# One step of a hybrid diffusion backbone: the stages of the mixer in another order

## The chip, the cores and the metric

The kernel runs on one core of a Trainium2 chip. The metric is the device time of one execution in microseconds (us). The kernel before takes 1578.61 us, the median of three runs from 1577.85 to 1579.18.

A core has engines that work side by side, each through its own instructions in order: TensorE (PE) multiplies matrices into PSUM banks, VectorE (DVE) and ScalarE (ACT) work element by element, GpSimd (POOL) and the queue engine SP here mostly issue DMAs. An instruction waits until what it reads has been written and what it overwrites has been read. ScalarE computes its functions (exponential, sigmoid, square root, gelu) from tables, and changes the table by an instruction of its own.

## The reference

Two layers of one network are applied to 128 context tokens and 256 latent tokens, 384 rows of 1024 numbers. Each layer is a feed-forward half step, a mixer and a second half step, each behind a norm that is scaled and shifted by numbers from a conditioning vector (the modulation):

```
mod = silu(cond) @ w_ada + b_ada
h = rmsnorm(x, g[0]) * (1 + mod[:, 1]) + mod[:, 0]
x = x + 0.5 * mod[:, 2] * swiglu(h, w_ffn_in[0], w_ffn_out[0])
h = rmsnorm(x, g[1]) * (1 + mod[:, 4]) + mod[:, 3]
x = x + mod[:, 5] * mixer(h)
h = rmsnorm(x, g[2]) * (1 + mod[:, 7]) + mod[:, 6]
x = x + 0.5 * mod[:, 8] * swiglu(h, w_ffn_in[1], w_ffn_out[1])
```

The mixer projects h (1024 columns) to 2144 columns, which three groups of heads share:

```
qa, ka, va, xb, gb, cq, ckv, kr = split(h @ w_in)        # 256 256 256 512 512 192 128 32
A: q, k = rope(headnorm(qa)), rope(headnorm(ka));  o_a = subln(softmax1 - lam * softmax2) @ va
B: xc = dwconv(xb); r, i = sigmoid(gates(xc)); a = exp(-8 r softplus(-lam))
   h_t = a_t h_(t-1) + sqrt(1 - a_t^2) i_t xc_t, forward and backward;  o_b = (hf + hb) * gelu(gb)
C: q = rope(headnorm(rmsnorm(cq) @ w_uq)); k, v from rmsnorm(ckv) @ w_ukv and kr;  o_c = softmax(q k) @ v
out = concat(o_a, o_b, o_c) @ w_out
```

Context tokens attend to context alone, latent ones to 128 cached context keys and the 256 latent keys. Normed keys, values, latents and the last scan states of the context are outputs too.

## The kernel before

The tokens lie as columns: x is eight tiles of 128 features by 384 tokens (xT). Products in full precision are made of three reduced ones (mm3, L474): high part times high part, high times low, low times high. Weights come as slabs (wslab, L457): SP loads a slab (tile wx, tag X, five buffers), ScalarE casts the high part (wh), VectorE subtracts for the low part (wl). The normed input of a stage is split likewise into hH and hL. Small products (gates psg, the heads psq and psk of group C, the modulation adaps) are plain 32-bit matmuls, and TensorE also transposes (pst, psT, psF).

The order on each engine is fixed when the program is built: a scheduler takes the instructions in the order of the code, moved by priorities (the table AHEAD), by what they need, and by a few written rules (`behind(a, b)`, an order without a wait). At run time no engine passes over a waiting instruction. PSUM has eight banks: four for projections and scores (pw), two p1, one p2, one pa; `turn` deals p1, p2, p1 in a circle.

A mixer (L832) goes through these stages in the code:

1. B's inputs, two halves of 256 columns (psw, the first half on the raw x, so that it can begin before the norm), and the convolution (xc).
2. B's scans, two halves: gates (psg, L891, sigmoid, tanh), exponentials, square roots, scans.
3. B's gelu projections (gb), A's values (psva, L953), then B's gate: gelu times scan, split to obH and obL (L962 to L967).
4. C's projection (psc, three banks), its norm (norm_c makes cl, which waits for all three banks) and its transposes (cT).
5. C's query heads (psq, heads_c makes yq, transposes, qh) and key heads (psk, yk, transposes, kC).
6. A's queries and keys (psa, norm_a makes ya; `stacked` packs high and low parts, stk; transposes make qS and kS).
7. Attention in twelve units: scores psS, exponential (prob), transposes psT, products with values psO. Between units an `out_pair` may compute the part of the output projection that needs B alone (the early pairs, 24 products po each); in layer 0 the modulation of the next stage is worked on (`ada.step`, adaps L368, weights adax loaded by POOL).
8. A's last norm, its transposes (psF) and the rest of the output projection.

`N_EARLY` says how many early pairs there are, `EARLY_STEP` how many units apart. The modulation products are placed behind the matmul of the stage's norm (`norm_last["pe"]`, L370).

Of the kernel before, what the change touches and what calls it, by code (L numbers as in the profile page):

```python
# [18 lines left out]
P = 128  # L19
D = 1024  # L20
KD = 8
# [17 lines left out]

N_RAW = [2, None, 2, 2, None, 2]  # L40

N_EARLY = [1, 1]
EARLY_STEP = [3, 2]
EARLY_AT = [0, 0]

LATE_F = 8
# [38 lines left out]
def hybrid_step_kernel(  # L85
# [257 lines left out]
    def ada_group(s, p, on_dve):  # L343
# [473 lines left out]
    def mixer(l, r_in, hs):  # L817
# [31 lines left out]
            held(wg[64 * b : 64 * b + 64, :, 64 * b : 64 * b + 64], wsrc[b])  # L849

        xcs = []
        for half in range(2):
            sl = in_slabs([(768 + 256 * half, 1024 + 256 * half)])
            for j in range(2):
                ch = 2 * half + j
# [22 lines left out]
                    V.scalar_tensor_tensor(xc, xp[:, jj : jj + TG], cw(jj), xc, ALU.mult, ALU.add)  # L878
                xcs.append(xc)


        lru = {}
        for half in range(2):
            chs = (2 * half, 2 * half + 1)
            for ch in chs:
                for dr in range(2):
# [22 lines left out]
            for ch in chs:  # L909
# [20 lines left out]
                        V.tensor_tensor(hsum, hsum, hh, ALU.add)  # L930
                lru[ch] = hsum

        gelus = []
        for half in range(2):
            sl = in_slabs([(1280 + 256 * half, 1536 + 256 * half)])
# [27 lines left out]
        for ch in range(4):  # L963
# [6 lines left out]
        pc = [PS("psc", "pw") for _ in range(3)]  # L970
        n_c = 352
        for q in range(4):
            h, lo = wslab([(W[q * 2 * P : (q + 1) * 2 * P, 1792:2144], 0)], 2, n_c, "in")
            for t in range(3):
                w0 = slice(t * P, (t + 1) * P)
                for kk in range(2):
                    xh, xl = hs[2 * q + kk]
                    o = pc[t][:, 0:n_c]
                    mm(o, xh[:, w0], h[:, kk, 0:n_c], start=(q + kk == 0), stop=False)
                    mm(o, xl[:, w0], h[:, kk, 0:n_c], start=False, stop=False)  # L980
                    mm(o, xh[:, w0], lo[:, kk, 0:n_c], start=False, stop=(q + kk == 4))
        cl = norm_c(l, pc)
        nc.gpsimd.dma_start(new_mla_ckv[0, l], cl[0][:, 192:320])
        nc.gpsimd.dma_start(new_mla_krope[0, l], cl[0][:, 320:352])
        cT = []
        for a, b in ((0, P), (P, P + 96), (192, 320)):
            ps = PS("pst", next(turn))
            for t in range(3):
                nc.tensor.transpose(ps[0 : b - a, t * P : (t + 1) * P], cl[t][:, a:b], ident)
            x = S("cT")  # L990
            nc.scalar.copy(x[0 : b - a, :], ps[0 : b - a, 0:T])
            cT.append(x)


        qk = []
        for t in range(3):
            ps = PS("psq", "pw")
            w0 = slice(t * P, (t + 1) * P)
            mm(ps[:, 0:T], cT[0][:, w0], uq[:, 0, :], start=True, stop=False)
            mm(ps[:, 0:T], cT[1][0:96, w0], uq[0:96, 1, :], start=False, stop=True)  # L1000
            qk.append((t, ps[:, 0:T].rearrange("p (h d) -> p h d", h=4), None))
        yq = heads_c(l, 0, qk)
        qh = {}
        for h in range(4):
            ps = PS("pst", next(turn))
            for t in range(3):
                nc.tensor.transpose(ps[0:96, t * P : (t + 1) * P], yq[t][:, h, :], ident)
            qh[h] = S("qh")
            nc.scalar.copy(qh[h][0:96, :], ps[0:96, 0:T])
        qk, vC_ = [], []  # L1010
        for t in (1, 2, 0):
            ps = PS("psk", "pw")
            mm(ps, cT[2][:, t * P : (t + 1) * P], ukv, start=True, stop=True)
            kv = ps.rearrange("p (h d) -> p h d", h=4)
            v = S("vC", (P, 256))
            nc.scalar.copy(v.rearrange("p (h d) -> p h d", h=4), kv[:, :, 64:128])
            vC_.append(v)
            qk.append((t, kv[:, :, 0:64], cl[t][:, 320:352]))
        vC_.insert(0, vc_c)
        yk = heads_c(l, 1, qk)  # L1020
        for h in range(4):
            ps = PS("pst", next(turn))
            for i in range(3):
                nc.tensor.transpose(ps[0:96, i * P : (i + 1) * P], yk[i][:, h, :], ident)
            nc.scalar.copy(kC[h][0:96, P:512], ps[0:96, 0:T])

# [120 lines left out]
            unit_pv(pair, *kind, e, *q)  # L1147

        ada.until(s, 2)

        kP = kp.tile([P, 8, P], F32R, name="kP", tag="K")
        places = (slice(0, 3, 2), 1), (slice(0, 2), 2)

        @placed("stk")
# [10 lines left out]
                out.append(sk.bitcast(F32))  # L1165
            return out

        def norm_a(kind, where):
            st = stats()
            for t in range(3):  # L1170
                sq = TT("sq", "sq", (P, 256))
                act(sq, where[t], AF.Square)
                V.reduce_sum(st[:, 0, 8 * t : 8 * t + 8], sq.rearrange("p (m d) -> p m d", m=8), axis=AX.X)
            V.tensor_scalar(st[:, 0, :], st[:, 0, :], 32 * EPS, None, op0=ALU.add)
            r = small_rsqrt(st, 24, 1.0 / 32)
            ys = []
            for t in (1, 2, 0):
                o = LT("ya", (P, 256))
                V.tensor_tensor(
                    o.rearrange("p (m d) -> p m d", m=8),  # L1180
                    where[t].rearrange("p (m d) -> p m d", m=8),
                    r[:, 8 * t : 8 * t + 8].unsqueeze(2).to_broadcast([P, 8, 32]),
                    ALU.mult,
                )
                ys.append(o)
            sks = []
            for t, o in zip((1, 2, 0), ys):
                y = o.rearrange("p (m d) -> p m d", m=8)
                gain_rotary(l, kind, t, y, 0, gains[:, l, G_A + 32 * kind : G_A + 32 * kind + 32], 8, 0)
                if kind == 1 and t == 0:  # L1190
                    nc.gpsimd.dma_start(new_diff_k[0, l].rearrange("t h c d -> t (h c d)"), o)
                sks.append(stacked(kind, o))
            return sks

        bank_p = PS("psa", "pw")
        last_p = None
        for kind in range(2):
            sl = in_slabs([(256 * kind, 256 * kind + 256)])
            bank_l = PS("psa", "pw")
            where = {0: bank_p[:, 256 * kind : 256 * kind + 256], 1: bank_l[:, 0:256], 2: bank_l[:, 256:512]}  # L1200
            for t in (1, 2, 0):
                w0 = slice(t * P, (t + 1) * P)
                after = last_p if t == 0 else last if t == 2 else None
                for k in range(KD):
                    h, lo = sl[k // HALF_K]
                    kk = k % HALF_K
                    xh, xl = hs[k]
                    o = where[t]
                    ins = mm(o, xh[:, w0], h[:, kk, :], start=(k == 0), stop=False)
                    if k == 0 and after is not None:  # L1210
                        behind(ins, after)
                    mm(o, xl[:, w0], h[:, kk, :], start=False, stop=False)
                    last = mm(o, xh[:, w0], lo[:, kk, :], start=False, stop=(k == KD - 1))
                if t == 0:
                    last_p = last
            sks = norm_a(kind, where)
            if kind == 0:
                sks = [sks[2], sks[0], sks[1]]
            else:
# [174 lines left out]
```

## Time and profile before

| | |
|---|---|
| median of three runs | 1578.61 us |
| the profiled run's own time | 1580.6 us |
| its span in the trace | 1578.8 us |
| TensorE busy | 1527.9 us, 97% |
| VectorE busy | 1113.6 us, 71% |
| ScalarE busy | 746.6 us, 47% |
| DMA, mean over the span | 158 GB/s |
| granted TensorE clock, mean | 0.99 |

The profiled run takes 1.8 us more than its span holds, and 2.0 us more than the median of the runs. Busy shares are averages over six stages; most of the span is the four feed-forwards, where matmuls stand without holes. The two mixers begin at 326.88 and 1095.87 us. A matmul's duration in a row includes its way through the array, so that neighbours overlap; the distance of two starts is what one costs. A plain 32-bit matmul leaves two records. A wait is shown in brackets behind the first instruction that had to wait, with what released it.

### The profile page before, as it was taken

What the parts mean: (1) busy time and instruction counts of PE and PEld (TensorE: products, weight loads), DVE (VectorE), ACT (ScalarE), POOL (GpSimd) and SP (SyncE); (2) the same over time, 40 slices, a digit from 0 to 9 for tenths busy, and PEclk for the clock granted to TensorE, in tenths of its full rate; (3) what the DMA queues carried; (4) which work ended last, traced back from release to release, by engine and by line L of the source; (5) the groups of instructions that cost most, each with busy time, mean ns of one, the idle gap of its engine ahead of it and who ended that gap; (6) DMA issues with size and microseconds to landing.
All of it is one profiled execution on the core that took longest, in us unless ns stands there. A gap on an engine that the chain in (4) does not pass through costs nothing.

```text
span 1578.8 us, 24260 instructions
## 1 busy us (share of the span) xinstructions
PE 1527.9 (97%) x9118; PEld 1441.2 (91%) x9118; DVE 1113.6 (71%) x2068; ACT 746.6 (47%) x1376; POOL 103.4 (7%) x194
## 2 busy tenths in 40 slices
PE   7999999999889999999999999999978999999998
PEld 5899999998668999999999999999857699999998
DVE  5888586587677988578578866777967789443332
ACT  4533332469577633333363333325975864333221
POOL 1202010001100001001000200110000000000000
PEclk9999999999999999999999999999989999999999
DMA  9978576523531587566537866674231046444341
GB/s 304 248 205 228 158 231 196 147 80 115 185 106 37 146 245 211 161 207 225 171 97 215 238 187 193 203 238 121 64 92 37 15 134 201 130 117 128 116 145 35
DMA packets 291034, 249.02 MB, mean 158 GB/s; under 512 B 11554, under 2 KB 273159, under 8 KB 290917
## 3 DMA queue, kind: packets, MB, share of 16 engines
q1 hardware_dynamic: 270224, 175.94, 38.2%
q0 software_dynamic: 20368, 71.34, 14.8%
q8 instruction: 71, 1.16, 0.3%
q14 instruction: 47, 0.38, 0.1%
q10 hardware_dynamic: 324, 0.20, 0.1%
HBM read 245.17 MB, written 2.27 MB: 157 GB/s over the span
## 4 chain that ended last, share of the span: by engine, by line
PE 88%; DVE 4%; ACT 4%; issue 2%; DMA 1%; POOL 0%; ACTq 0%; DVEq 0%; POOLq 0%
PE po L475 9%; PE po L476 9%; PE po L477 9%; PE pg L475 8%; PE pg L477 8%; PE pg L476 8%; PE pu L475 8%; PE pu L477 8%; PE pu L476 8%; PE psw L476 1%; PE psg L891 1%; PE psw L475 1%; PE psw L477 1%; PE adaps L378 1%; ACT gate L143 1%
## 5 line engine op out<-in xcount | busy, mean ns | idle before, releaser
L471 DVE TENSOR_TENSOR wl<-wx,wh 128x1024 fp32r<-128x1024 f32 (+2 forms) x332 | 385.4, 1163 | 302.8 <-ACT wh L470 294.3
L470 ACT CAST wh<-wx 128x1024 fp32r<-128x1024 f32 (+2 forms) x332 | 333.2, 1005 | 448.5 <-PE po L476 237.3
L362 DVE SCALAR_TENSOR_TENSOR ada<-adax,sc,ada 128x1024 f32<-128x1024 f32 x196 | 244.2, 1280 | 17.8 <-DMA adax<-in_w_ada_dram 17.4
L475 PE MATMUL po<-aH,wh 128*128 128x384 f32 x704 | 239.7, 341 | 0.0
L477 PE MATMUL po<-aH,wl 128*128 128x384 f32 x704 | 237.7, 338 | 0.0
L476 PE MATMUL po<-aL,wh 128*128 128x384 f32 x704 | 237.2, 337 | 0.0
L475 PE MATMUL pg<-hH,wh 128*128 128x384 f32 x640 | 216.9, 339 | 0.0
L475 PE MATMUL pu<-hH,wh 128*128 128x384 f32 x640 | 216.2, 338 | 0.0
L477 PE MATMUL pg<-hH,wl 128*128 128x384 f32 x640 | 215.9, 337 | 0.2 <-DVE wl L471 0.2
L477 PE MATMUL pu<-hH,wl 128*128 128x384 f32 x640 | 215.6, 337 | 0.0
L476 PE MATMUL pu<-hL,wh 128*128 128x384 f32 x640 | 215.5, 337 | 0.0
L476 PE MATMUL pg<-hL,wh 128*128 128x384 f32 x640 | 215.4, 337 | 0.0
L143 ACT ACTIVATE sg<-pg 128x384 f32<-128x384 f32 x80 | 39.4, 493 | 206.5 <-PE pg L477 206.5
L475 PEld LDWEIGHTS po<-aH,wh 128*128 128x128 f32 x704 | 132.4, 188 | 3.9 <-issue 2.1
L476 PEld LDWEIGHTS po<-aL,wh 128*128 128x128 f32 x704 | 132.2, 188 | 0.5 <-issue 0.5
L477 PEld LDWEIGHTS po<-aH,wl 128*128 128x128 f32 x704 | 132.2, 188 | 0.0
L354 POOL DMA_DIRECT2D adax<-in_w_ada_dram x128 | 68.1, 533 | 892.3 <-DVE ada L360 466.5
L475 PEld LDWEIGHTS pg<-hH,wh 128*128 128x128 f32 x640 | 120.2, 188 | 2.5 <-issue 2.1
L477 PEld LDWEIGHTS pg<-hH,wl 128*128 128x128 f32 x640 | 120.1, 188 | 0.6 <-DVE wl L471 0.5
L476 PEld LDWEIGHTS pg<-hL,wh 128*128 128x128 f32 x640 | 120.2, 188 | 0.0
L475 PEld LDWEIGHTS pu<-hH,wh 128*128 128x128 f32 x640 | 120.2, 188 | 0.0
L477 PEld LDWEIGHTS pu<-hH,wl 128*128 128x128 f32 x640 | 120.1, 188 | 0.0
(327 smaller groups left out, 2425.9 us busy)
## 6 DMA issues: line engine op xcount, KB each, us to landing
wx<-in_w_ffn_in_dram SPq DMA_DIRECT2D x352, 256.0 KB, 4.1
adax<-in_w_ada_dram POOLq DMA_DIRECT2D x128, 512.0 KB, 4.9
wx<-in_w_ffn_out_dram SPq DMA_DIRECT2D x80, 512.0 KB, 3.9
wx<-in_w_in_dram SPq DMA_DIRECT2D x28, 512.0 KB, 3.8
adax<-in_w_ada_dram SPq DMA_DIRECT2D x16, 512.0 KB, 7.7
wx<-in_w_ffn_out_dram SPq DMA_DIRECT2D x16, 256.0 KB, 3.3
wx<-in_w_out_dram SPq DMA_DIRECT2D x8, 512.0 KB, 3.9
wx<-in_w_out_dram SPq DMA_DIRECT2D x16, 256.0 KB, 2.7
```

The source lines that it names most:

```text
L143: ins = nc.scalar.activation(out, in_, func, **kw)
L354: nc.gpsimd.dma_start(x, w_ada[l, k * P : (k + 1) * P, c0 : c0 + D])
L362: ins = V.scalar_tensor_tensor(accs[c], x, w, accs[c], ALU.mult, ALU.add)
L378: mm(bank[32 * a : 32 * a + 32, 256 * c : 256 * c + 256], cm(C_ONE, n1=32), x[:, a], start=True, stop=True)
L470: nc.scalar.copy(h[:, 0:nk, 0:ncol], x[:, 0:nk, 0:ncol])
L471: V.tensor_tensor(lo[:, 0:nk, 0:ncol], x[:, 0:nk, 0:ncol], h[:, 0:nk, 0:ncol].bitcast(F32), ALU.subtract)
L475: mm(out, wh, xh, start=first, stop=False)
L476: mm(out, wh, xl, start=False, stop=False)
L477: last_mm[0] = mm(out, wl, xh, start=False, stop=last)
L891: mm(ps[:, 0:TG], wg[:, wi, :], xcs[ch], start=True, stop=True)
```

## The change

The code of the mixer's stages is put in another order: B's input half 0; C's projection, norm and transposes; B's input half 1; B's scans half 0; A's queries and keys with their norm; C's heads; B's scans half 1; the gelu projections; A's values; B's gate; then stacking, transposes and attention. A's normed heads are now kept in one tile per kind (ya, tag YA, two buffers, 6 KB per partition in all), and the slab pool loses a fifth buffer for wx. psq and psk take their banks from `turn` instead of pw, and are ordered behind the last A product. Two early output pairs instead of one stand between the units, three units apart. The modulation products are ordered behind the latest three-part product (`last_mm[0]`) instead of the norm's matmul.

```diff
-N_EARLY = [1, 1]
-EARLY_STEP = [3, 2]
+N_EARLY = [2, 2]
+EARLY_STEP = [3, 3]
...
-    wp = ctx.enter_context(tc.tile_pool(name="wp", bufs=5))
+    wp = ctx.enter_context(tc.tile_pool(name="wp", bufs=4))
...
                     ins = mm(bank[32 * a : 32 * a + 32, 0:256], sc[:, k, :], x[:, a], start=(k == 0), stop=(k == KD - 1))
-                    if norm_last["pe"] is not None:
-                        behind(ins, norm_last["pe"])
+                    behind(ins, last_mm[0])
...
         xcs = []
-        for half in range(2):
+
+        def b_input(half):
...
+        b_input(0)
+
+
+        pc = [PS("psc", "pw") for _ in range(3)]
...
+        cl = norm_c(l, pc)
...
+        b_input(1)
+
 
         lru = {}
-        for half in range(2):
+
+        def b_scan(half):
...
+        b_scan(0)
+
+        def norm_a(kind, where):
...
+            ya = kp.tile([P, 3, 256], F32, name="ya", tag="YA", bufs=2)
+            for t in (1, 2, 0):
+                V.tensor_tensor(
+                    ya[:, t, :].rearrange("p (m d) -> p m d", m=8),
...
+        yas = []
+        bank_p = PS("psa", "pw")
...
+            yas.append(norm_a(kind, where))
...
+            ps = PS("psq", next(turn))
...
+            behind(ins, last)
...
+        yq = heads_c(l, 0, qk)
...
+            ps = PS("psk", next(turn))
...
+            behind(ins, last)
...
+        yk = heads_c(l, 1, qk)
+        for h in range(4):
+            ps = PS("pst", next(turn))
+            for i in range(3):
+                nc.tensor.transpose(ps[0:96, i * P : (i + 1) * P], yk[i][:, h, :], ident)
+            nc.scalar.copy(kC[h][0:96, P:512], ps[0:96, 0:T])
+
+        b_scan(1)
+
+
         gelus = []
...
         for kind in range(2):
...
+            sks = [stacked(kind, yas[kind][:, t, :]) for t in (1, 2, 0)]
```

On ScalarE in layer 1, from the copies of C's keys (kC) to the first exponential (prob), the kernel before has these rows (stk are A's stacked heads, wh weights, qS and kS the transposed stacks):

```order
L1025 COPY kC<-pst 96x384 x4
L143 ACTIVATE nst<-nst 128x24
L1163 CAST stk<-ya 128x4x2x32 x2
L470 CAST wh<-wx 128x512
L1163 CAST stk<-ya 128x4x2x32 x4
L143 ACTIVATE sq<-psa 128x256 x3
L1226 CAST qS<-pst 96x384 x8
```

After the change there stand, behind the same copies, the second half of the scans (gate, th), of which this is the beginning, and at its end the rows of the second fence:

```order
L1057 COPY gb<-psw 128x384 x4
L1046 COPY kC<-pst 96x384 x4
L143 ACT_TABLE_LOAD
L143 ACTIVATE gate<-psg,vA 128x387 x2
L143 ACTIVATE th<-gate,u_half 128x387
```

The stack, the gelu and the split of B's output (obH) follow the scans on the same engine:

```order
L143 ACTIVATE th<-th 128x387 x3
L1075 COPY vA<-psva 128x256 x3
L1221 CAST stk<-ya 128x4x2x32 x6
L1221 CAST stk<-ya 128x4x64 x6
L1221 CAST stk<-cdk 128x4x64 x2
L143 ACT_TABLE_LOAD
L143 ACTIVATE gb<-gb 128x384 x3
L453 CAST obH<-hscan 128x384
```

So the scans' second half, the values' copies and B's gate moved from ahead of C's heads to a place between those heads and the transposed stacks.

On TensorE in layer 1, at the beginning of attention, the kernel before has scores, transposes and products with values one behind the other:

```order
L1053 MATMUL psS<-kP,qS 128x128 x2
L1088 MATMUL psO<-pT,vc_c 64x128
L1079 MATMUL psT<-kc_76,prob 128x128 x2
L1088 MATMUL psO<-pT,vc_c 64x128
L1088 MATMUL psO<-pT,vC 64x128 x4
L1079 MATMUL psT<-kc_76,prob 128x128 x4
L1065 MATMUL psS<-kC,qh 128x128 x2
```

After the change the second early output pair (po, 24 products) begins there; five more rows of it are shown:

```order
L1148 MATMUL psO<-pT,vC 64x128 x4
L1139 MATMUL psT<-kc_76,prob 128x128 x5
L474 MATMUL po_12433<-obH,wh 128x384
L475 MATMUL po_12433<-obL,wh 128x384
L476 MATMUL po_12433<-obH,wl 128x384
L474 MATMUL po_12434<-obH,wh 128x384
L475 MATMUL po_12434<-obL,wh 128x384
L1148 MATMUL psO<-pT,vc_c 64x128
```

The other 19 of the pair follow within the next rows; behind the last product of attention six output products now stand ahead of psF, where 27 stood.

In layer 0 the modulation products (adaps) stand on TensorE, in before, in groups at C's projection, at its transposes, at psk and at A's projections; this is the group at the transposes of cl:

```order
L981 MATMUL psc<-wl,hH 128x352
L368 MATMUL adaps<-adax,sc 32x256 x18
L989 MATMUL pst<-kc_76,cl 128x128
L368 MATMUL adaps<-adax,sc 32x256 x2
L989 MATMUL pst<-kc_76,cl 128x128
```

After the change all 64 lie in attention, in groups of one to five:

```order
L476 MATMUL po_4554<-obH,wl 128x384
L368 MATMUL adaps<-adax,sc 32x256 x5
L1125 MATMUL psS<-kC,qh 128x384 x2
L1139 MATMUL psT<-kc_76,prob 128x128
L368 MATMUL adaps<-adax,sc 32x256 x3
L1125 MATMUL psS<-kC,qh 128x384
```

So they moved from the stages ahead of attention into it.

## Rows read from the trace of the kernel before

**Rows 1.** Windows of five stretches: start:end, us, busy (records) by engine, clock, DMA.
```profile
326.88:457.65 130.77, 121.82 (x786) 99.49 (x785) 102.65 (x265) 97.11 (x210) 15.06 (x29) 0.99 0.42 134
457.65:496.40 38.75, 35.72 (x231) 27.48 (x232) 31.14 (x112) 30.31 (x107) 0.00 (x0) 0.96 0.03 9
1095.87:1227.46 131.59, 114.98 (x658) 98.33 (x657) 100.85 (x256) 97.21 (x210) 6.34 (x12) 0.95 0.23 70
1227.46:1262.92 35.46, 32.61 (x226) 24.84 (x227) 30.82 (x112) 30.56 (x107) 0.00 (x0) 1.00 0.00 1
1262.92:1290.00 27.08, 27.08 (x157) 26.76 (x157) 23.23 (x62) 17.51 (x32) 0.00 (x0) 1.00 0.46 134
```

**Rows 2.** Windows holding only psw, psc, psa, and po after a wait.
```profile
1102.00:1106.00 4.00, 4.00 (x25) 4.00 (x24) 4.00 (x13) 3.07 (x7) 0.00 (x0) 1.00 0.00 0
1162.80:1166.82 4.02, 4.02 (x26) 4.02 (x26) 4.02 (x9) 3.17 (x13) 0.15 (x1) 1.00 0.76 217
1201.24:1207.52 6.28, 6.28 (x56) 6.28 (x54) 5.22 (x16) 2.30 (x8) 0.00 (x0) 1.00 0.30 86
1213.70:1217.60 3.90, 3.90 (x13) 3.90 (x14) 3.89 (x11) 0.71 (x2) 0.54 (x1) 0.56 0.15 49
```

**Rows 3.** Waits of PE, 1095.87 to 1227.46: us in total, times, longest.
```profile
PE pst L989 <- ACT cl L143: 6.5, 1, 6.5
PE po L475 <- DVE ya L1179: 2.2, 1, 2.2
PE psk L1013 <- DVE yc L755: 2.0, 1, 2.0
PE pst L1224 <- DVE stk L1164: 1.6, 2, 1.5
```

**Rows 4.** Timeline of PE, layer 1: start us, duration us, instruction, records [wait].
```profile
1118.01 1.46 PE L891 MATMUL psg<-xc,wg 128*128 128x387 f32 x4
...
1184.72 1.98 PE L1013 MATMUL psk<-ukv,cT 128*128 128x512 f32 x4 [2.04 <-DVE yc L755]
...
1208.39 3.14 PE L1224 MATMUL pst<-kc,stk 128*96 128x128 f32 x24 [0.15 <-DVE stk L1164]
...
1267.18 0.38 PE L1121 MATMUL psF<-kc,o 128*128 128x128 f32 x2
...
1268.93 0.96 PE L475 MATMUL po<-oaH,wh 128*128 128x384 f32 x4
```

**Rows 5.** Timeline of ACT, layer 1.
```profile
1140.03 1.28 ACT L143 ACT_TABLE_LOAD   x1
1141.33 1.06 ACT L143 ACTIVATE gate<-psg,vA 128x387 f32<-128x387 f32 x2
...
1155.68 1.34 ACT L143 ACTIVATE th<-th 128x387 f32<-128x387 f32 x3
...
1190.99 0.99 ACT L143 ACTIVATE hsq<-psk 128x256 f32<-128x256 f32 x3
...
1199.87 1.62 ACT L1025 COPY kC<-pst 96x384 f32<-96x384 f32 x4 [0.41 <-PE pst L1024]
...
1223.02 3.14 ACT L1226 CAST kS<-pst 96x384 fp32r<-96x384 f32 x8 [1.00 <-PE pst L1224]
...
1227.46 0.37 ACT L143 ACTIVATE prob<-psS,st 128x128 f32<-128x128 f32 x1
```

**Rows 6.** Groups of ACT, 1095.87 to 1227.46: busy us, mean ns.
```profile
L1163 ACT CAST stk<-ya 128x256 fp32r<-128x256 f32 x12 | 4.1, 403 | 6.6 <-DVE ya L705 6.6
...
L143 ACT ACTIVATE gb<-gb 128x384 f32<-128x384 f32 x4 | 1.8, 512 | 0.0
```

**Rows 7.** Timeline of PE, layer 0, at the transposes of cl.
```profile
403.27 0.64 PE L368 MATMUL adaps<-adax,sc 128*32 128x256 f32 x8 [3.67 <-DMA adax<-in_w_ada_dram]
```

**Rows 8.** DMA issues of the page: count, KB each, us to landing.
```profile
wx<-in_w_ffn_in_dram SPq DMA_DIRECT2D x352, 256.0 KB, 4.1
adax<-in_w_ada_dram POOLq DMA_DIRECT2D x128, 512.0 KB, 4.9
```

More of the change, by code (lines that the diff above doesn't have):

```diff
@@ L931, in mixer @@
                 lru[ch] = hsum
+        b_scan(0)
+        def norm_a(kind, where):
+            st = stats()
+            for t in range(3):
+                sq = TT("sq", "sq", (P, 256))
+                act(sq, where[t], AF.Square)
+                V.reduce_sum(st[:, 0, 8 * t : 8 * t + 8], sq.rearrange("p (m d) -> p m d", m=8), axis=AX.X)
+            V.tensor_scalar(st[:, 0, :], st[:, 0, :], 32 * EPS, None, op0=ALU.add)
+            r = small_rsqrt(st, 24, 1.0 / 32)
+            ya = kp.tile([P, 3, 256], F32, name="ya", tag="YA", bufs=2)
+            for t in (1, 2, 0):
+                V.tensor_tensor(
+                    ya[:, t, :].rearrange("p (m d) -> p m d", m=8),
+                    where[t].rearrange("p (m d) -> p m d", m=8),
+                    r[:, 8 * t : 8 * t + 8].unsqueeze(2).to_broadcast([P, 8, 32]),
+                    ALU.mult,
+                )
+            for t in (1, 2, 0):
+                y = ya[:, t, :].rearrange("p (m d) -> p m d", m=8)
+                gain_rotary(l, kind, t, y, 0, gains[:, l, G_A + 32 * kind : G_A + 32 * kind + 32], 8, 0)
+            if kind == 1:
+                nc.gpsimd.dma_start(new_diff_k[0, l].rearrange("t h c d -> t (h c d)"), ya[:, 0, :])
+            return ya
@@ new lines, in mixer @@
+        yas = []
+        bank_p = PS("psa", "pw")
+        last_p = None
+        for kind in range(2):
+            sl = in_slabs([(256 * kind, 256 * kind + 256)])
+            bank_l = PS("psa", "pw")
+            where = {0: bank_p[:, 256 * kind : 256 * kind + 256], 1: bank_l[:, 0:256], 2: bank_l[:, 256:512]}
+            for t in (1, 2, 0):
+                w0 = slice(t * P, (t + 1) * P)
+                after = last_p if t == 0 else last if t == 2 else None
+                for k in range(KD):
+                    h, lo = sl[k // HALF_K]
+                    kk = k % HALF_K
+                    xh, xl = hs[k]
+                    o = where[t]
+                    ins = mm(o, xh[:, w0], h[:, kk, :], start=(k == 0), stop=False)
+                    if k == 0 and after is not None:
+                        behind(ins, after)
+                    mm(o, xl[:, w0], h[:, kk, :], start=False, stop=False)
+                    last = mm(o, xh[:, w0], lo[:, kk, :], start=False, stop=(k == KD - 1))
+                if t == 0:
+                    last_p = last
+            yas.append(norm_a(kind, where))
@@ new lines, in mixer @@
+        qk = []
+        for t in range(3):
+            ps = PS("psq", next(turn))
+            w0 = slice(t * P, (t + 1) * P)
+            ins = mm(ps[:, 0:T], cT[0][:, w0], uq[:, 0, :], start=True, stop=False)
+            behind(ins, last)
+            mm(ps[:, 0:T], cT[1][0:96, w0], uq[0:96, 1, :], start=False, stop=True)
+            qk.append((t, ps[:, 0:T].rearrange("p (h d) -> p h d", h=4), None))
+        yq = heads_c(l, 0, qk)
+        qh = {}
+        for h in range(4):
+            ps = PS("pst", next(turn))
+            for t in range(3):
+                nc.tensor.transpose(ps[0:96, t * P : (t + 1) * P], yq[t][:, h, :], ident)
+            qh[h] = S("qh")
+            nc.scalar.copy(qh[h][0:96, :], ps[0:96, 0:T])
@@ new lines, in mixer @@
+        qk, vC_ = [], []
+        for t in (1, 2, 0):
+            ps = PS("psk", next(turn))
+            ins = mm(ps, cT[2][:, t * P : (t + 1) * P], ukv, start=True, stop=True)
+            behind(ins, last)
+            kv = ps.rearrange("p (h d) -> p h d", h=4)
+            v = S("vC", (P, 256))
+            nc.scalar.copy(v.rearrange("p (h d) -> p h d", h=4), kv[:, :, 64:128])
+            vC_.append(v)
+            qk.append((t, kv[:, :, 0:64], cl[t][:, 320:352]))
+        vC_.insert(0, vc_c)
@@ L933, in mixer @@
+        yk = heads_c(l, 1, qk)
+        for h in range(4):
+            ps = PS("pst", next(turn))
+            for i in range(3):
+                nc.tensor.transpose(ps[0:96, i * P : (i + 1) * P], yk[i][:, h, :], ident)
+            nc.scalar.copy(kC[h][0:96, P:512], ps[0:96, 0:T])
+        b_scan(1)
         gelus = []
@@ L967, in mixer @@
             o_b.append(split(lru[ch], "ob", pool=LT))
[L970 to L992, printed above, removed]
@@ L995, in mixer @@
[L995 to L1025, printed above, removed]
@@ L1149, in mixer @@
         ada.until(s, 2)
-        kP = kp.tile([P, 8, P], F32R, name="kP", tag="K")
         places = (slice(0, 3, 2), 1), (slice(0, 2), 2)
@@ L1166, in stacked @@
             return out
[L1168 to L1193, printed above, removed]
@@ L1195, in mixer @@
-        bank_p = PS("psa", "pw")
-        last_p = None
-        for kind in range(2):
[L1198 to L1216, printed above, removed]
+        kP = kp.tile([P, 8, P], F32R, name="kP", tag="K")
```

20 lines of the change are left out of this document (added).

## The prediction, made blind

> **What bounds the kernel now.** I read the windows first, stretch by stretch. In the mixer of layer 1 the 131.59 us from its first norm matmul to the first softmax exponential hold 114.98 us of TensorE, 100.85 of VectorE and 97.21 of ScalarE [rows 1]: no engine is full, TensorE has no matmul in 16.6 us, and what ends there is a chain that hands work from one engine to the next. Layer 0 is alike, 130.77 us. The attention stretch has 32.61 of 35.46 us on TensorE and 30.8 and 30.6 on the two others; the 27.08 us behind it are TensorE without a hole. The waits say where the 16.6 us are: 6.5 for the normed C projection, 2.2 and 1.6 for A's rotated and stacked heads, 2.0 for a PSUM bank that VectorE still reads [rows 3]. Dense matmuls stand 0.174 us apart at 384 columns (4.00 us, 25 records, two of which lap in), 0.168 at 352 and 0.116 at 256 [rows 2]. Outside the mixers order and work stay as they are, so the sum is over two mixers.
>
> **A. Up to the first exponential.** The change fills the wait for the C norm (6.5 us) with B's second input half and gates, and takes A's projections away from the end, so all waits of [rows 3], 12.3 us, lose their place. What is late next? In the new order on ScalarE the key copies kC stand directly ahead of B's second half of scans, then follow A's value copies, the stacking, B's gate, both sets of stacked transposes, and only then the exponential. In before, 26.0 us lie between the end of kC (1199.87 + 1.62) and the exponential at 1227.46 [rows 5]. The new chain, term by term: the second half of scans took 17.0 us (table load at 1140.03 to the last square root, 1155.68 + 1.34) [rows 5]; 14 stacking casts at 4.1/12 are 4.8 [rows 6]; the gelu table load is 1.3, four gelus and four casts of the same tile at 1.8/4 are 3.6 [rows 5, 6]; qS and kS copies 3.1 each, the exponential's load 1.3, and five more copies and casts at 1.62/4 are 2.0 [rows 5]. Together 36.2 us, all on one engine that works in order. VectorE works behind each step; I assume it is no later than in before.
>
> When is kC done? TensorE's work up to psk: 174 products of 384 columns (48 raw, 126 others) x 0.174 = 30.3; 72 of 352 x 0.168 = 12.1; 144 of 256 x 0.116 = 16.7; 17 plain fp32 products (8 gates, 6 psq, 3 norm) at about 0.7, since two gates took 1.46, = 11.9; psk 2.9, three at 1.98/2; 21 transposes at 3.14/24 = 2.7 [rows 2, 4]. That is 76.6 us. New waits stand in it: the third bank of the C projection must be released by B's first input; cl is still waited for, though later matmuls cover most; weights come in a new order; the q heads are needed for their transposes. Bounds 4 and 12 (the sum of the four old ones is 12.3), taken 7. From the end of psk (1184.72 + 1.98) to the end of kC it was 14.8 us; from the first square of the k heads (1190.99) 10.5 [rows 4, 5]; in the new order the q heads' copies, which filled the difference, are past, but value copies, gelu copies and weight casts stand there: I take 12. So kC ends at 76.6 + 7 + 12 = 95.6, the exponential starts at 131.8: against 131.6 and 130.8, **+0.6 us** per mixer. Bounds: 76.6 + 4 + 10.5 + 36.2 = 127.3 and 76.6 + 12 + 14.8 + 36.2 = 139.6, so -3.9 to +8.4; if the waits inside the old 17.0 us of scans go too, some 2 us less, -5.9.
>
> So the waits removed come back as one long hole: behind psk TensorE has only 18 products of psw, 72 of A's values, 8 gates and 21 transposes, 3.1 + 8.4 + 5.6 + 2.7 = 19.8 us, while the first obH, which the early output products need, comes 12 + 17 + 2 + 4.8 + 1.3 + 2, about 39 us, behind psk.
>
> What does that do to the clock? After the 2.2 us wait for ya, output products ran under a granted clock of 0.56, 13 records in 3.90 us, 0.3 us apart, where dense ones take 0.174 [rows 2, 3]: 1.2 GHz against 2.4. The Trainium skill, "TensorE: Matmul & The Clock Gate", section "What's actually happening", says that the throttled state is the default and that activity lifts it; the trace agrees, and the rule speaks against this change, which trades several short holes for one of 19 us. By the rule 24 early products would cost 3.0 us more (24 x 0.126) where they end last; by the order they end beside ScalarE's copies, so I put 0 in the sum and leave this to the third rival.
>
> One rule would lengthen the chain. The second scan half's first activation starts at 1141.33, 0.02 us behind the end of its table load (1140.03 + 1.28) [rows 5]. The Trainium skill, "ScalarE: Activation LUTs", section "What ACT_TABLE_LOAD costs", gives about 1283 ns and 1380 ns of drain for each switch. By the page the chain's five loads would add 6.9 us to the 36.2; the trace has the 1.28 and no drain behind it, so the measurement decides.
>
> **B. Attention.** A second pair of early output columns (24 products, 4.2 us at 0.174) now stands almost in one block among the transposes of the first units, with its residual on VectorE. TensorE works in order, so the softmax chain behind waits for it. The stretch has 2.85 us without a matmul on TensorE [rows 1]. From 0 (in the holes) to 7.2 (24 x 0.3 at half clock); I take half of 4.2, **+2.1** per mixer.
>
> **C. The tail.** From the last product of attention (1262.92, where the window ends) to the transposes of A's output (1267.18) and to the first products on them (1268.93) it is 6.0 us [rows 1, 4]. In before output products fill this; after, 6 stand there and 120 behind. So 6.0 + 120 x 0.174 = 26.9 against 27.08 [rows 1], **-0.2**; at half clock again up to +1.6.
>
> **D. Modulation products in layer 0.** 64 of them were spread over the stages from C's projection to the first early output products, where they also waited for their loads (3.67 us in the longest) [rows 7]. They took no time: layer 0, with them, is 0.8 us shorter up to the exponential than layer 1, without them [rows 1]. Now they are ordered behind the latest three-part product and all stand between the softmax units. Four took 0.64 us, 64 some 8 to 10; each load of 512 KB takes 4.9 us [rows 7, 8]. From -3 (the earlier stages come free of them) to +8 (all in line); taken **+2**, nearer the hole of 3.0 us that layer 0's attention has (38.75 less 35.72).
>
> **E. Four slab buffers for five.** In a feed-forward a slab feeds 24 products, 4.2 us, and lands in 4.1 [rows 8]; four in a row are 16.7 us ahead. 0 to 4.1 (one landing laid bare at the start), taken **+0.3**.
>
> **Sum.** 2 x (0.6 + 2.1 - 0.2) + 2 + 0.3 = +7.3 on the profiled run's 1580.6. That run lies 2.0 above the median of 1578.61, so 1585.9: **1586 us**. A difference below 0.2% (3.2 us) can't be told from none.
>
> **Rivals.**
> Faster (chance 0.35): the new waits are few, kC is done at 91, the scans of the second half run denser than before since nothing else disturbs them: -4 to -6 per mixer. The second early pair falls into holes (0), the tail gives 0.2, the modulation products -1. That is 2 x -5.2 - 1, about -11: 1567 us. For it: 16.6 us without a matmul, which B's gates and A's projections can fill; against it: the 36 us on ScalarE, where now nothing runs beside but 20 us of TensorE. It decides if kC ends before 93 us from the mixer's start.
> No change (0.17): A gives 3 us per mixer, B and D take as much: 1578.6.
> Much slower (0.10): the hole leaves TensorE at half clock into attention, the 24 products take 7.2, the modulation products queue for their loads with two waits like the 3.67, the tail +1.6: 2 x (4 + 6 + 1.6) + 8, over 1600.
> My forecast (0.38): 1582 to 1598, its own range; the chain on ScalarE is as long as what it replaces and attention pays for the block.
>
> Faster 0.35, same 0.17, slower 0.48. The range of 8 in 10 is 1564 to 1598: the bounds of A (2 x -5.9), with B and C at their best and D at -3 reach -15; above, the last 1 in 10 stays out.
>
> **What would show it.** Right: kC ends 94 to 98 us after the norm's first matmul, ScalarE is then busy to the exponential for 35 to 38 us, the exponential comes at 130 to 134; TensorE shows one wait of over 10 us for obH or for a scan; attention is 37 to 39 us in layer 1 and 40 to 43 in layer 0. Wrong: the exponential before 128 us, by a chain of under 33 us or a kC before 92; attention no longer than before with 24 more products in it; a wait for wx in the feed-forwards over 2 us in all; modulation products without waits.

## The result and the profile after

The changed kernel takes 1622.2 us (median of four runs, 1621.0 to 1628.0) against 1578.2 of before in the same comparison: ratio 1.0285, 95% interval 1.026 to 1.031. It is slower by 44 us, where 7 were forecast and 1598 was the upper end.

The windows of the same stretches, in the profile after; columns as in [rows 1]. The first three are layer 0, up to the first exponential, attention, and the rest; the next three the same of layer 1; the last two are stretches named below.

```profile
328.40:465.80 137.40, 115.53 (x663) 99.61 (x662) 99.35 (x255) 97.17 (x210) 6.65 (x13) 0.91 0.23 68
465.80:520.90 55.10, 53.49 (x379) 34.85 (x374) 37.44 (x128) 32.32 (x109) 8.64 (x16) 0.97 0.55 168
520.90:549.00 28.10, 24.42 (x134) 23.70 (x132) 22.23 (x61) 16.23 (x31) 0.00 (x0) 0.94 0.39 112
1121.50:1260.60 139.10, 116.31 (x655) 100.48 (x653) 98.83 (x252) 97.23 (x209) 6.39 (x12) 0.90 0.23 67
1260.60:1302.90 42.30, 39.15 (x255) 30.46 (x256) 34.57 (x121) 32.00 (x110) 0.00 (x0) 1.00 0.06 20
1302.90:1332.40 29.50, 25.82 (x134) 25.13 (x134) 22.77 (x62) 16.23 (x31) 0.00 (x0) 0.88 0.37 107
1182.50:1186.40 3.90, 3.90 (x12) 3.90 (x13) 3.76 (x12) 0.22 (x1) 0.00 (x0) 0.50 0.66 177
1247.80:1253.80 6.00, 5.99 (x22) 5.58 (x23) 3.98 (x9) 3.78 (x9) 0.00 (x0) 0.62 0.35 114
```

Against [rows 1]: up to the exponential 6.6 us more in layer 0 (137.40 for 130.77) and 7.5 in layer 1 (139.10 for 131.59); attention 16.4 more in layer 0 and 6.8 in layer 1. From the end of attention to the next stage's first matmul it was 26.9 and 27.2 us, and is 28.1 and 29.5. Mixer by mixer that is 24.2 and 16.6, nearly all of the 42.2 by which the span grew; the four feed-forwards keep their lengths to 0.3 us, but for 1.1 in the first. ScalarE's work up to the exponential is the same (97.2 us). TensorE's is 1.3 us more in layer 1, but it is without a matmul for 22.8 us there (139.10 less 116.31) where it was 16.6; in layer 0 for 21.9 where it was 9.0.

The waits of TensorE in layer 1 up to the exponential, which answer to [rows 3]:

```profile
PE psw L476 <- DVE wl L470: 5.3, 1, 5.3
PE pst L1237 <- DVE stk L1222: 4.8, 1, 4.8
PE pst L1045 <- DVE yc L704: 3.4, 1, 3.4
PE psS L1125 <- ACT vA L1075: 3.3, 1, 3.3
PE po L474 <- ACT obH L453: 1.9, 1, 1.9
PE psva L1071 <- ACT gb L1057: 1.4, 1, 1.4
PE pst L903 <- ACT cl L143: 0.7, 1, 0.7
```

The 6.5 us for cl fell to 0.7, as meant, but new ones came: all waits of this stretch, the small ones that are not shown too, are 22.2 us for 16.3 in before, 12.3 of these in [rows 3]. The timeline of ScalarE from the key copies to the exponential (answers to [rows 5]):

```profile
1221.35 0.47 ACT L1046 COPY kC<-pst 96x384 f32<-96x384 f32 x1 [0.17 <-PE pst L1045]
1221.84 1.28 ACT L143 ACT_TABLE_LOAD   x1
...
1236.78 1.34 ACT L143 ACTIVATE th<-th 128x387 f32<-128x387 f32 x3
1238.03 0.89 ACT L1075 COPY vA<-psva 128x256 f32<-128x256 f32 x3
1238.81 3.78 ACT L1221 CAST stk<-ya 128x256 fp32r<-128x256 f32 x12
...
1247.25 0.51 ACT L453 CAST obH<-hscan 128x384 fp32r<-128x384 f32 x1 [1.39 <-DVE hscan L1084]
...
1254.15 2.01 ACT L1239 CAST qS<-pst 96x384 fp32r<-96x384 f32 x5 [2.57 <-PE pst L1237]
1256.06 3.28 ACT L1239 CAST kS<-pst 96x384 fp32r<-96x384 f32 x8
1259.36 1.28 ACT L143 ACT_TABLE_LOAD   x1
1260.65 0.37 ACT L143 ACTIVATE prob<-psS,st 128x128 f32<-128x128 f32 x1
```

ScalarE works on without a wait of over 0.3 us but for two, 38.8 us from 1221.82 to the exponential. The second wait is TensorE's: the early output pair (the last of the windows above) stands ahead of the remaining transposes for qS. TensorE had 2.7 us of matmuls in the 9.8 us ahead of the pair, and the pair's first 20 products took 6.0 us under a granted clock of 0.62.

### The profile page after: what moved, and what is told of

The parts are those of the page before. It is cut to its first block, busy times and chain, and to the rows that moved or that the text cites. A ratio compares the mean times of both kernels' runs of the same rounds, so it can differ in the third digit from the quotient of the medians.

```text
span 1621.0 us, 24294 instructions
## 1 busy us (share of the span) xinstructions
PE 1544.0 (95%) x9118; PEld 1452.3 (90%) x9118; DVE 1116.7 (69%) x2076; ACT 746.5 (46%) x1376; POOL 103.5 (6%) x194
## 4 chain that ended last, share of the span: by engine, by line
PE 85%; DVE 6%; ACT 4%; issue 3%; DMA 2%; POOL 0%; SPq 0%; POOLq 0%; DVEq 0%; ACTq 0%
PE po L474 9%; PE po L475 9%; PE po L476 9%; PE pg L476 8%; PE pg L475 8%; PE pg L474 8%; PE pu L476 8%; PE pu L475 8%; PE pu L474 7%; DMA adax<-in_w_ada_dram 2%; ACT gate L143 1%; PE psg L921 1%; ACT L143 1%; PE psw L476 1%; PE psw L474 1%
```

## The experiments

Two theories stood at first. Theory 1: attention is bound by TensorE, so what is put in lengthens it one for one, and a clock at half rate behind waits counts where TensorE ends last. Theory 2: the parts only cost in company, or by something else than their length. Both are put anew for each question. Times are medians of 4 to 12 runs, with a profile of each kernel; before ran at 1578.6 to 1580.8 beside them.

**One part undone at a time.** `a_ada_back` and `a_one_early`, and both together, `a_order_only`:

```diff
-                    behind(ins, last_mm[0])
+                    if norm_last["pe"] is not None:
+                        behind(ins, norm_last["pe"])
```

> The changed kernel (1622.2 us), only the modulation products of layer 0 back behind the norm's matmul. Theory 1 (attention is bound by TensorE, so what is put into it lengthens it one for one): the 64 products leave attention, which in layer 0 falls from 55.1 to 44 to 46 us; the holes ahead of attention take them: about 1612. Theory 2 (they cost by waiting for their loads, wherever they stand): attention shorter, the part ahead longer by as much, 1618 to 1622.

```diff
-N_EARLY = [2, 2]
-EARLY_STEP = [3, 3]
+N_EARLY = [1, 1]
+EARLY_STEP = [3, 2]
```

> The changed kernel with one early output pair instead of two (units apart as in before). Theory 1: attention falls by 4 to 6 us in each layer (24 products less), the hole of 3.2 us ahead of psF is filled again and the half clock behind it goes, 2 us per layer: about 1608. Theory 2 (attention is longer because its tiles and banks come in another order, the pair fits the holes): 1618 to 1622.

> The changed kernel with both undone (one early pair, modulation products behind the norm): the new order of the stages with four slab buffers and nothing else. Theory 1: the two gains add up, 1622 - 10 - 14 = about 1598, and what is left over 1578, some 14 to 20 us, lies ahead of the first exponential (131.6 and 130.8 us before, 139.1 and 137.4 after). Theory 2: under 5 us less than 1622.

Measured 1614.1, 1604.5 and 1598.8 us (ratios to before 1.022 [1.019, 1.0245], 1.015 [1.013, 1.018], 1.012 [1.010, 1.0135]). So the second pair costs 15 to 18 us, the modulation products 6 to 8, the order by itself 20. Attention in windows, layer 0 and layer 1, of the three in this order:

```profile
465.40:508.90 43.50, 40.56 (x258) 30.87 (x258) 35.56 (x123) 31.63 (x110) 0.00 (x0) 1.00 0.06 19
1247.20:1294.00 46.80, 43.79 (x255) 34.02 (x256) 34.77 (x121) 32.34 (x110) 0.00 (x0) 0.89 0.06 18
```

```profile
463.30:510.80 47.50, 47.41 (x351) 29.50 (x351) 34.58 (x122) 31.44 (x108) 8.66 (x16) 1.00 0.61 184
1248.30:1284.50 36.20, 33.47 (x229) 25.32 (x229) 32.09 (x115) 30.90 (x108) 0.00 (x0) 1.00 0.02 8
```

```profile
467.70:505.60 37.90, 35.00 (x236) 26.59 (x236) 32.98 (x117) 30.55 (x108) 0.00 (x0) 1.00 0.06 21
1243.60:1279.80 36.20, 33.49 (x229) 25.32 (x229) 32.11 (x115) 30.94 (x109) 0.00 (x0) 1.00 0.03 9
```

With one pair and no modulation products attention is about as long as before (38.75 and 35.46 in [rows 1]); in layer 0 the modulation products alone make it 9.6 us longer (47.5 for 37.9), and the pair alone 5.6 (43.5 for 37.9). TensorE's busy time, the first engine's in each line, says how. The pair added 5.6 us of TensorE's work (40.56 for 35.00) and used none of its idle time, 2.9 us with and without it. The modulation products added 12.4 (47.41 for 35.00), and of the 2.9 us 0.1 was left. So theory 1 holds, with the prices 5.6 for 24 products that take 4.2 when dense, and 9.6 for 64. Why the pair takes more than when dense is not shown. The modulation products are not free ahead of attention in the new order either: the exponential of layer 0 comes at 142.2 us with them and at 139.3 without.

**The same parts put into the old order.** `b_ada_early2`: the kernel before with these two edits reversed.

> The kernel before, in its old order and with five slab buffers, with two early pairs three units apart and the modulation products behind the latest three-part product. Theory 1: attention longer by 6 in layer 1 and 15 in layer 0, the hole ahead of psF open, its time ahead of attention as before: 1598 to 1602. Theory 2 (these parts cost only together with the new order): 1578 to 1584.

1607.7 us, ratio 1.018 [1.016, 1.020], 29 us over before, where the two parts cost 23 in the new order (1622.2 less 1598.8). The exponential is where it was (132.0 and 130.6 us), attention 51.4 and 44.9:

```profile
456.50:507.90 51.40, 50.58 (x362) 32.69 (x361) 36.14 (x124) 31.91 (x108) 7.60 (x14) 1.00 0.51 156
1239.20:1284.10 44.90, 41.41 (x251) 32.30 (x252) 33.44 (x116) 31.90 (x109) 0.00 (x0) 0.92 0.03 8
```

The two parts need no new order to cost, and theory 2 falls for them. In layer 1 the granted clock was 0.92 there and 1.00 in the profile after (42.30 us); I put the 2.6 us between the two down to that.

**The 20 us of the order.** Theory 1 was now that what ScalarE does behind the key copies sets the end. `o_scan1_early` is the order alone with one line moved:

```diff
+        b_scan(1)
+
         qk = []
         for t in range(3):
             ps = PS("psq", next(turn))
...
-        b_scan(1)
```

> The new order alone (1598.8 us), with B's second half of scans ahead of C's heads instead of behind them. Theory 1 (what ScalarE has to do between the key copies and the first exponential sets the end; that was 39 us): 17 us leave this stretch and fill ScalarE's idle 20 us ahead of it; the exponential comes at 125 to 133 us of the mixer instead of 139 to 142, 1570 to 1585. Theory 2 (the holes of TensorE in the middle, above all the 5.3 us for the split of the gelu weights, and the half clock behind them set it): the key copies come as much later as the stretch gets shorter, 1594 to 1600.

1605.4 us, ratio 1.017 [1.015, 1.019]: slower still by 6. The stretch from kC to the exponential did fall, from 39.7 to 21.4 us, and kC came at 120.0 for 99.6: the query heads now stood behind the scans, and TensorE had nothing else. Its longest waits:

```profile
PE pst L1030 <- DVE yc L707: 11.3, 1, 11.3
PE psw L477 <- DVE wl L471: 4.9, 1, 4.9
PE psva L1071 <- ACT gb L1057: 2.4, 1, 2.4
```

So the chain behind kC alone doesn't set the end: my theory fell. `o_in300` moves the splits of weights ahead of the scans' steps:

```diff
-AHEAD = {"in": 120, ...
+AHEAD = {"in": 400, ...
```

> The new order alone, with the splits of the mixer's weight slabs 400 places ahead instead of 120, so that those of the gelu weights stand amid the first half of scans. Theory 2: the 5.3 us wait falls under 1.5 and the exponential comes 4 to 6 us earlier per mixer, 1587 to 1591. Theory 1 allows for at most that, since the 39 us behind the key copies stay; if the scans are delayed by the splits instead, 1596 to 1600.

1593.3, ratio 1.008 [1.007, 1.010]: layer 1's exponential at 135.0 for 139.3. The 5.3 us for wl went, and 4.5 us for a bank that A's norm still read took their place; behind it the clock was at half again. `o_warm` fills waits in layer 1 with matmuls without use (here the first of three places):

```diff
+        def warm(n, after):
+            for i in range(n):
+                ins = mm(warm_ps[:, 0:T], hs[0][0][:, 0:P], hs[1][0], start=True, stop=True)
+                behind(ins, after)
+                after = ins
+            return after
...
+        w1 = warm(30, last_2) if l else None
```

> The new order alone (1598.8 us), and in layer 1 matmuls without use in three waits of TensorE: 30 ahead of the gelu projections (wait 5.3 us), 30 ahead of the stacked transposes (3.3 and 4.8 us), 8 ahead of the early output pair (1.9 us). They only keep TensorE at work; the output stays. Theory 1 (the half clock behind the waits costs, since the early pair at 0.3 us a product stands ahead of the transposes): the pair takes 3.5 us for 6, the first exponential of layer 1 comes at 134 to 136.5 us for 139.3, 1594 to 1597. Theory 2 (only the hand-overs count): 138.5 to 140, 1598 to 1600.

1594.0, ratio 1.008 [1.0065, 1.010]; layer 1's exponential at 135.6, and the first early products ran at a granted clock of 1.00 (0.62 in after):

```profile
1227.74:1233.00 5.26, 3.47 (x19) 2.79 (x19) 4.70 (x10) 3.78 (x8) 0.00 (x0) 1.00 0.37 115
```

That the 3.7 us are the clock's alone is not shown: with the edit the scheduler also put other instructions elsewhere. The first copy of A's values came 101.3 us into the mixer for 116.4, and the 3.3 us wait for vA is gone too. Do the two edits add?

> The new order alone with both edits of before: splits of the weights 400 places ahead, and matmuls without use in three waits of layer 1. Theory 1 (the first exponential is late by the wait for the gelu weights and by the half clock behind it and behind the wait for obH, and these are two things): layer 1 from 139.3 us to 130.5 to 132.5, where before is (131.6); with one of the edits alone it came at 135.0 and 135.6. Theory 2 (both edits act on the same 4 us): 134 to 136. In time 1586 to 1590 or 1591 to 1595.

1592.7, ratio 1.008 [1.007, 1.009], the exponential at 134.6: they do not. Both act on the same 4 us. The other 3 of layer 1 are none of the two; that they are the waits behind psk for other engines' results is argued, not shown. `o_gate_late` (B's gate behind the stacked transposes):

```diff
-        o_b = []
-        for ch in range(4):
...
+        o_b = []
+        for ch in range(4):
...
         for n_, (fn, e, q) in enumerate(units):
```

> The new order alone, with B's gate (gelu, product, split) behind the stacked transposes instead of ahead of them, so that the early output pair no longer stands ahead of these on TensorE. Theory 1 (what ScalarE and TensorE still have to do behind the key copies sets the first exponential): from 39.7 us to 34 to 37, the exponential 3 to 5 us earlier per mixer; the early pair goes on into attention: 1590 to 1596. Theory 2 (waits only change places): 1597 to 1601.

1601.0, ratio 1.014 [1.012, 1.016]. The exponential comes at 135.8, 3.5 us earlier, and attention, which now holds the pair, takes 41.2 for 36.2. Given back with interest.

**Does the early C projection gain by itself?** `b_c_first` and `b_c_earlier` move that block alone, in the kernel before (to `lru = {}` and to `gelus = []`):

```diff
+        pc = [PS("psc", "pw") for _ in range(3)]
...
+            cT.append(x)
+
         lru = {}
```

> The kernel before with one move: C's projection, norm and transposes ahead of B's scans instead of behind B's gate; both halves of the scans stay ahead of the gelu projections and of C's heads. Theory 1 (the early C projection by itself is a gain, since the 6.5 us wait for cl goes and nothing is put behind the key copies): the exponential at 124 to 128 us, 1565 to 1573. Theory 2 (another hole opens, the part is bound by its total of hand-overs): 1576 to 1580.

> As the one before, but C's projection, norm and transposes stand behind B's scans and ahead of the gelu projections. Theory 1: 1567 to 1574, by the wait for cl. Theory 2: 1576 to 1580.

1588.1 and 1604.8, ratios 1.004 [1.003, 1.006] and 1.0155 [1.014, 1.017]: both slower, theory 1 is wrong. The waits of the first, in layer 1, and below them the longest of the second:

```profile
PE psk L1013 <- DVE yc L755: 9.5, 1, 9.5
PE po L475 <- DVE ya L1179: 4.9, 1, 4.9
PE psq L999 <- ACT vA L982: 3.5, 1, 3.5
```

```profile
PE pst L952 <- ACT cl L143: 13.7, 1, 13.7
```

In the first the 6.5 us for cl are gone, and 9.5 for yc (2.0 in [rows 3]), 4.9 for ya (2.2) and 3.5 for a bank stand there. As I read it, the heads' chain had C's own products as work ahead of it and lost them. In the second the wait for cl did not go at all: it is 13.7 us. `v2_a_in_cl_wait` tried A's projections as the filling, in the old order of everything of B, with four slab buffers and A's heads in tiles of their own as in after (the stages stand for their code, and the lines compare with before):

```diff
-b_input(0), b_input(1), b_scan(0), b_scan(1), gelu, values, gate, C, C heads, A
+b_input(0), b_input(1), b_scan(0), b_scan(1), gelu, values, gate, C, A, C heads
```

> The stages of the kernel before with one exchange: A's queries and keys with their norm directly behind C's projection, ahead of C's transposes and heads, instead of behind these; everything of B stays ahead of both. (Four slab buffers, A's heads in their own tiles, stacking behind C's heads.) Theory 3 (a hole of TensorE is the shadow of a chain on ScalarE and VectorE; it is only saved where independent matmuls are at hand and nothing else loses its cover): A's 144 products fill the 6.5 us for cl; behind them only C's heads (some 19 us of chain), copies and casts are left, while ScalarE does the stacking: the first exponential at 117 to 125 us, 1556 to 1568. Rival (the heads' chain loses the cover it had, A's products): 129 to 133 us, 1575 to 1583.

1580.0, ratio 1.0001 [0.999, 1.002]: no change, the rival's case. In layer 1 the wait for cl went, and the heads wait 6.2 and 6.8 us:

```profile
PE pst L1085 <- DVE yc L705: 6.8, 2, 5.2
PE pst L1068 <- DVE yc L707: 6.2, 1, 6.2
```

The exponential comes at 129.3 us (131.6), but attention takes 38.5 us with the pair inside. `v2e_pair_in_hole` puts that pair into the wait:

```diff
         yq = heads_c(l, 0, qk)
+        out_pair(0, [(2, 4)], o_b, False)
...
-            if rest == 0 and 0 <= m < N_EARLY[l]:
-                out_pair(2 * m, [(2, 4)], o_b, False)
```

> A's projections directly behind C's (1580.0 us, and 38.5 us of attention in layer 1 with the early output pair at its beginning), with that pair moved into the wait for the query heads, between psq and their transposes, where TensorE has nothing else for 11 us and obH has long been there. Theory 3 (products cost nothing where no other work is at hand, and their full length in attention): the first exponential stays at 129 to 132 us, attention falls to 35 to 36, 1572 to 1576. Rival (the pair delays the heads, or attention stays long by its own chain): 1579 to 1582.

Attention of layer 1 in the two kernels:

```profile
1224.50:1263.00 38.50, 36.35 (x249) 28.61 (x248) 33.19 (x118) 31.13 (x109) 0.00 (x0) 1.00 0.03 8
```

```profile
1230.70:1266.20 35.50, 32.97 (x227) 24.98 (x227) 31.11 (x114) 30.42 (x108) 0.00 (x0) 1.00 0.01 1
```

In layer 1 as expected: 3.0 us less, the exponential 0.9 later, the mixer 192.8 us for 194.9. In time not: 1587.0, ratio 1.004 [1.003, 1.006], since in layer 0 the exponential came at 137.6 us for 131.7; there the modulation products stand in the same holes, and what of them delays the heads was not tried apart. Last, does the half clock cost in the kernel before? `b_warm` puts 36 matmuls without use into the wait for cl in layer 1:

```diff
+        if l:
+            warm_ps = PS("warm", "pa")
+            for i in range(36):
+                ins = mm(warm_ps[:, 0:T], hs[0][0][:, 0:P], hs[1][0], start=True, stop=True)
+                behind(ins, last_c)
+                last_c = ins
```

> The kernel before with 36 matmuls without use in layer 1 where TensorE waits 6.5 us for cl. Theory 1: the transposes and head products behind it run dense (psq 0.65 us each, not 1.3), the first exponential of layer 1 comes 2 to 4 us earlier: 1575 to 1577. Theory 2 (the heads' chain on the other engines ends last there, not TensorE): within 1 us of before.

1578.1, ratio 0.999 [0.998, 1.0003]: the exponential 2.5 us earlier (129.1), attention 39.1 us in its profile for 35.5, and no gain that can be told:

```profile
1224.60:1263.70 39.10, 36.64 (x226) 28.53 (x227) 31.01 (x112) 30.85 (x108) 0.00 (x0) 0.87 0.01 1
```

This is the clean test of the half clock: up to the exponential ScalarE and VectorE have the same instructions in the same order as in before, and on TensorE, besides the added ones, three transposes moved. The psk end, kC and the exponential all come 2.5 us earlier, so the half clock behind the wait for cl cost 2.5 us there. In the profiled run, 1581.4 us, attention gave them back: the same 226 records as in [rows 1] ran at a granted clock of 0.87 for 1.00. The seven of the twelve runs with a mean granted clock of 0.994 to 0.996 took 1575.1 to 1578.3 us, the five with 0.990 to 0.992 1578.9 to 1583.0. No version beat the kernel before.

## Why the prediction was wrong

It had the side right and the size wrong by 36 us. Up to the exponential it was 14.1 us more in the two mixers together where 1.2 were forecast (A); attention was 23.2 more for 6.2 (B and D); the stretches behind attention 3.5 more for 0.4 less (C). Its steps in turn:

- **B, attention.** Forecast +2.1 per mixer, measured 6.8 in layer 1, and 15 to 18 us in time for both with the tail. The failed step: "The stretch has 2.85 us without a matmul on TensorE", taken as room for half of the block. TensorE was busy 92% of that stretch [rows 1], and the pair filled none of the rest: in layer 1 3.15 us without a matmul are left (42.30 less 39.15), in `a_ada_back` 2.9 in layer 0. The block goes onto TensorE's own time in full. The upper bound of 7.2 came near the number by luck: it took the 24 products at half clock, and they cost 6.8 in layer 1 under a granted clock of 1.00.
- **D, modulation products.** Forecast +2, measured 6 to 8 in time, 9.6 in attention of layer 0. "Nearer the hole of 3.0 us" was right in kind, for these small products did fill 2.8 us of it; wrong was the size of what goes in, 12.4 us of TensorE's work for 64 products, where "64 some 8 to 10" was the estimate (64 x 0.16 is 10.2) and +8 the bound. They waited only once for a load; the mechanism is length, not loads:

```profile
PE adaps L368 <- DMA adax<-in_w_ada_dram: 1.6, 1, 1.6
```

- **C, the tail.** Forecast -0.2, measured +1.2 and +2.3. The wait ahead of psF is 3.2 us, and the stretch with the 120 products behind it shows a granted clock of 0.94 and 0.88, in before 1.00 in layer 1. The prediction had the half clock as its upper end, +1.6; layer 1 is beyond it.
- **A.** Forecast +0.6, measured 6.6 and 7.5, inside its bounds. In layer 1 the exponential came at 139.1 us for 131.8. The waits up to psk are 7.5 us (7 were taken). TensorE's work up to psk took 80.2 us for 76.6: behind the longest wait it ran at half rate until 1187.6 us (0.50 in the window from 1182.50), which I estimate at 2.5 of these 3.6, and the "dense" price of every product left no room for that. So psk ended at 87.7 us for 83.6. From psk to kC it was 12.6 (12), and kC ended at 100.3 us for 95.6. The chain on ScalarE took 38.8 for 36.2. Its own work was a little shorter than the sum, 34.9; the failed step is "VectorE works behind each step; I assume it is no later than in before", with TensorE taken the same way: 1.4 us went to a product that VectorE had not done, 2.6 to the transposes behind the half-rate pair. For the half clock of that pair the prediction said "I put 0 in the sum", since the products would end beside ScalarE's copies; the qS copies waited for them. What the clock cost of the 7.3 us is not separated: `o_warm` gained 3.7 in layer 1 with other instructions moved too, and `b_warm` 2.5 behind one wait in the kernel before. By the rule of the Trainium skill that the prediction weighed ("TensorE: Matmul & The Clock Gate", "What's actually happening": throttled by default, released by activity) the pair would have cost the prediction's estimate of 3.0 more; the trace agrees with the rule, with 20 products in 6.0 us where 0.174 each makes 3.5. One reading was off without weight: 26 records in 4.02 us [rows 2] are 0.161 us apart and not 0.168, 0.5 us less for C's 72 products.
- **E.** Forecast +0.3: the feed-forwards kept their lengths to 0.3 us, the first to 1.1; in the other kernels with four buffers the first stage took 304.4 to 307.5 us, in before 306.7. Five buffers in the new order were not tried.
- **The rivals and the range.** "Much slower" had 0.10 and "over 1600". Its number came true, its mechanism in part: the tail at half clock did; but the 24 products cost their length in attention at nearly full clock (1.00 and 0.97), and the modulation products did not queue for loads. The doubtful terms were treated as if each could fall either way by itself. Here A to D all lay above their forecast, and as I read it they have one cause: work put in front of an engine that is the bound, or behind a wait. The prediction's own upper bounds add up to 46.5 us (2 x (8.4 + 7.2 + 1.6) + 8 + 4.1), 1625; the range was closed at 1598 without a row for it. None of the signs for "right" came: kC was later than 98 us, the exponential than 134, no single wait was over 10, attention was longer.

What the order's remaining loss is, the runs show in this form: a hole of TensorE ahead of attention did not go in any of eight arrangements, it changed its name (cl 6.5 in before; then wl 5.3 and stk 4.8; yc 11.3; yc 9.5 and ya 4.9; cl 13.7; yc 6.2 and 6.8). The time without a matmul up to the first exponential of layer 1 was 15.4 to 27.0 us in them, 16.6 in before, and the exponential came between 129.3 and 142.8 us. The new order alone puts the exponential of layer 1 at 139.3 us for 131.6; which wait makes the 3 of these 7.7 us that neither `o_in300` nor `o_warm` took away is open. Layer 0 was taken apart no further than the modulation products.

## What to carry to other kernels

In these runs a block of products among a chain of small steps cost its full length and more where TensorE was over nine tenths busy, whatever the idle time added up to; small single products used the idle time, but only as much of it as there was. In layer 1 a pair no longer lengthened attention when it stood in one hole of 6.2 us instead, and the exponential came 0.9 us later (`v2e_pair_in_hole`). Where a wait went, another came at the place that the work moved into it had covered before (6.5 us for cl, then 6.2 and 6.8 for yc): so before moving a block, list which later wait it hides where it stands. And behind each wait of some microseconds put the half clock into the sum, if other engines wait for TensorE's next products: 2.5 us behind the 6.5 us wait here (`b_warm`).

## What the runs showed of the hardware

The clock also fell where TensorE waited for no more than 0.6 us at a time. The same 255 matmul records of layer 1's attention, in the same order, took 42.3 us at a granted clock of 1.00 in the profile after and 46.8 at 0.89 in that of `a_ada_back`. There the clock fell to half for some 10 us:

```profile
1269.40:1279.70 10.30, 10.30 (x45) 7.98 (x44) 6.12 (x21) 5.63 (x17) 0.00 (x0) 0.50 0.01 2
```

Just ahead of it stand two waits of 0.54 and 0.52 us; in after the same two, 0.53 and 0.51 us at 1280.9 and 1282.3, left the clock at 1.00. The Trainium skill, "TensorE: Matmul & The Clock Gate", section "A second HAM failure mode: psum-queue depth-cycling", tells of short idles between groups of matmuls that let the clock swing; the two windows agree with it, but what let it fall in one run and not in the other is not shown. The spread of the runs goes with the clock: of the four of `a_ada_back` the shortest, 1610.6 us, had a mean granted clock of 0.980, the longest, 1618.9 us, 0.975.

A change of ScalarE's table costs the load alone here as well: 1.28 us, and in `after` the load at 1259.36 is followed by the exponential at 1260.65, 0.01 us behind its end.
